# A RoPE kernel: rows of 16 KB instead of 64 KB where the DMA queue first goes over from loads to stores

## The chip, the cores and the metric

One core of one Trainium2 chip. The metric is the device time of one execution in microseconds (us), as the median of several runs. Lengths of rows are counted on the fp32 side (HBM) unless bf16 is said.

## The reference

```python
x: (8, 2048, 16, 64) fp32; cos, sin: (2048, 32) fp32
x1, x2 = x_pairs[..., 0], x_pairs[..., 1]        # neighbours along the last axis
out1 = x1 * cos - x2 * sin
out2 = x1 * sin + x2 * cos
out = stack([out1, out2], -1).reshape(x.shape)   # fp32
```

Eight batches, each 8 MB in and 8 MB out. There is little arithmetic for each byte.

## The kernel before

Each partition holds 16 consecutive sequence positions (`K = 16`) of a batch, 1024 elements each, so one partition's part of a batch is one contiguous run of 64 KB in HBM. Loads cast fp32 to bf16 and stores cast back. Every big transfer is issued by GpSimd, and they all go through one software queue, in the order of issue. There are three load buffers and three store buffers.

```python
P, K, KP, NX, NO, HEAD, TAIL = 128, 16, 8, 3, 3, 2, 4
x_t   = x.rearrange("b (p k) h d -> b p k (h d)", p=P, k=K)
out_t = out.rearrange("b (p k) h d -> b p k (h d)", p=P, k=K)

def load(b, k0=0):
    if b not in xs:
        xs[b] = xpool.tile([P, K, HD], bf16, name="xt")
    nc.gpsimd.dma_start(out=xs[b][:, k0:], in_=x_t[b, :, k0:])

def store(b, k1=K):
    nc.gpsimd.dma_start(out=out_t[b, :, :k1], in_=os[b][:, :k1])

# ... start: two positions of batch 0 and the tables by the other queues, then
load(0, HEAD)
load(1)
# ... tables are expanded on VectorE
load(2)
for b in range(B):
    os[b] = opool.tile([P, K, HD], bf16, name="ot")
    for k0 in range(0, K, KP):
        rotate(b, k0, k0 + KP)          # three tensor_tensor on VectorE
    if b + NX < B:
        load(b + NX)
    store(b, K if b < B - 1 else K - TAIL)
# ... the last four positions of the last batch leave by another queue
```

So the queue holds four loads (L0 to L3), then S0, L4, S1, L5, S2, L6, S3, L7, S4, S5, S6, S7. A place where a load is followed by a store is called a turn below; L3 to S0 is the first in this kernel. Each of the 16 DMA engines carries 8 partitions, which are 8 rows of 64 KB in each load or store.

## Time and profile before

| | before |
|---|---|
| median of 3 runs (range) | 317.47 us (317.31 to 317.48) |
| span of the profiled run | 315.7 us |
| VectorE busy | 212.8 us, 67% |
| DMA engines busy with the software queue | 97.0% |
| HBM bytes read and written over the span | 427 GB/s |

These are lines of the page of the kernel before: busy time by engine, the DMA rows of the 40 slices (a 9 means at least 90% busy), and one line of the queue table.

```profile
DVE 212.8 (67%) x51; ACT 6.9 (2%) x4; POOL 8.8 (3%) x20
...
DMA  9999999999999999999999999999999999999996
GB/s 269 212 246 203 199 212 253 199 199 237 361 465 332 199 257 407 399 332 262 203 399 440 357 199 199 482 448 266 199 316 415 399 399 523 407 399 457 423 434 280
...
q0 software_dynamic: 2304, 98.04, 97.0%
```

The DMA engines never rest, and VectorE does. The bytes are given, so all that can be won is time in which the engines are busy without moving data at their rate. To find such time, look at the table of stretches. Its columns are: the stretch and its length in us, the busy time of VectorE, ScalarE and GpSimd with the number of instructions, the granted clock, and then the two that matter here, the DMA share and the GB/s. **How to read these two:** a packet (one row) is counted with its whole length in the stretch in which it begins. If the stretch is one cadence long (2.40 us, the time from the start of one row to the start of the next) and one row of each engine begins in it, then share times length is the mean length of these rows. GB/s counts the bf16 side of a load and the fp32 side of a store, so 218 and 437 are the same speed.

```profile
core 0: us, DVE busy (x) ACT busy (x) POOL busy (x), PEclk, DMA share, GB/s
76.10:78.50 2.40, 2.40 (x2) 0.00 (x0) 0.00 (x0) 1.00 1.01 218
78.50:80.90 2.40, 2.40 (x1) 0.00 (x0) 1.05 (x2) 1.00 1.32 218
80.90:81.70 0.80, 0.80 (x1) 0.00 (x0) 0.00 (x0) 1.00 0.00 0
118.00:120.40 2.40, 2.40 (x2) 0.00 (x0) 0.00 (x0) 1.00 1.01 218
120.40:122.80 2.40, 2.37 (x2) 0.00 (x0) 0.00 (x0) 1.00 1.02 437
```

The seventh row of L3, which begins at about 76 us, takes 1.01 × 2.40 = 2.42 us, as all rows do. Its eighth and last takes 1.32 × 2.40 = 3.17 us, and where the next packets should begin, from 80.9 to 81.7 us, none does. That is 0.74 us lost per engine at the first change from loads to stores. At the next such change (L4 to S1, at about 120.4 us) the last row of the load takes 2.42 us again.

The list of issues and landings says the same. Its last column is the time from issue to landing; the load was issued at 52.20 us and the store at 52.72 us, so they landed at 82.8 and 102.2 us.

```profile
xt<-in_x_dram POOLq DMA_DIRECT2D x1, 4096.0 KB, 30.6
out_dram<-ot POOLq DMA_DIRECT2D x1, 49.5
```

### The profile page before, as it was taken

The numbers are of one execution on the slowest core, as the hardware profiler recorded it, in microseconds if no ns is written. First come the engines' busy times: TensorE is split into PE (matmuls) and PEld (weight loads), VectorE is DVE, ScalarE is ACT, GpSimd is POOL, SyncE is SP. The second block draws the span as 40 slices with busy tenths as digits, with TensorE's granted clock in tenths as the row PEclk, the third lists the DMA queues.
The fourth block names the chain that finished last, engine by engine and source line by source line (L and its number), as shares of the span: only waits on it lengthen the run. The fifth ranks groups of instructions, "written<-read, shape, count | busy, mean of one in ns | idle before, by whom it ended". The sixth has DMA issues, their size and how long they took to land.

```text
span 315.7 us, 146 instructions
## 1 busy us (share of the span) xinstructions
DVE 212.8 (67%) x51; ACT 6.9 (2%) x4; POOL 8.8 (3%) x20
## 2 busy tenths in 40 slices
DVE  0009999999999999619992299913999049990000
ACT  2100000000000000000000000000000000000400
POOL 1000001000100100100001000000000000000000
DMA  9999999999999999999999999999999999999996
GB/s 269 212 246 203 199 212 253 199 199 237 361 465 332 199 257 407 399 332 262 203 399 440 357 199 199 482 448 266 199 316 415 399 399 523 407 399 457 423 434 280
DMA packets 3024, 101.71 MB, mean 322 GB/s; under 512 B 336, under 2 KB 336, under 8 KB 848
## 3 DMA queue, kind: packets, MB, share of 16 engines
q0 software_dynamic: 2304, 98.04, 97.0%
q1 hardware_dynamic: 432, 2.88, 2.4%
q10 hardware_dynamic: 288, 0.79, 0.6%
HBM read 67.63 MB, written 67.11 MB: 427 GB/s over the span
## 4 chain that ended last, share of the span: by engine, by line
another core or an unknown queue 61%; DMA 16%; DVE 9%; ACT 1%; issue 0%; POOL 0%; ACTq 0%
DMA out_dram<-ot 16%; DVE xt L76 3%; DVE ot L81 3%; DVE ot L75 3%; ACT xt L117 1%; DVE c_tab L100 0%; POOL xt L57 0%; ACTq L116 0%; ACT ot L116 0%; ACTq L117 0%
## 5 line engine op out<-in xcount | busy, mean ns | idle before, releaser
L75 DVE TENSOR_TENSOR ot<-xt,c_tab 128x8192 bf16<-128x8192 bf16 x16 | 70.7, 4420 | 45.8 <-DMA out_dram<-ot 45.7
L81 DVE TENSOR_TENSOR ot<-ot,xt 128x8192 bf16<-128x8192 bf16 x16 | 70.8, 4425 | 0.5
L76 DVE TENSOR_TENSOR xt<-xt,s_tab 128x8192 bf16<-128x8192 bf16 x16 | 70.8, 4425 | 0.5
L98 DVE CAST s_tab<-xt 128x512 bf16<-128x512 f32 x1 | 0.5, 454 | 23.8 <-DMA xt<-in_sin_dram 23.8
L57 POOL DMA_DIRECT2D xt<-in_x_dram x8 | 4.4, 547 | 161.4 <-DVE ot L81 137.4
L60 POOL DMA_DIRECT2D out_dram<-ot x8 | 4.3, 535 | 113.8 <-DVE ot L81 113.8
L116 ACT COPY ot<-ot 1x1 bf16<-1x1 bf16 x1 | 0.2, 193 | 286.6 <-DMA out_dram<-ot 286.6
L117 ACT CAST xt<-ot 128x4096 f32<-128x4096 bf16 x1 | 3.6, 3604 | 0.0
L96 ACT CAST xt<-xt 128x2048 bf16<-128x2048 f32 x1 | 1.9, 1897 | 0.0
L96 ACT ACT_TABLE_LOAD x1 | 1.3, 1283 | 5.7 <-DMA xt<-in_x_dram 5.7
L100 DVE CAST c_tab<-xt 128x1024 bf16<-128x1024 f32 x1 | 0.7, 683 | 0.0
L99 DVE TENSOR_SCALAR s_tab<-xt 128x512 bf16<-128x512 f32 x1 | 0.4, 442 | 0.0
L133 POOL MEMSET const-float32-0.0<- 128x1 f32 x1 | 0.1, 98 | 0.2 <-issue 0.2
L133 POOL MEMSET const-bfloat16-1.0<- 128x1 bf16 x1 | 0.1, 101 | 0.0
L133 POOL MEMSET const-float32-1.0<- 128x1 f32 x1 | 0.1, 98 | 0.0
L133 POOL MEMSET const-uint8-127<- 128x1 uint8 x1 | 0.1, 98 | 0.0
## 6 DMA issues: line engine op xcount, KB each, us to landing
xt<-in_x_dram POOLq DMA_DIRECT2D x7, 4096.0 KB, 42.8
out_dram<-ot POOLq DMA_DIRECT2D x1, 6144.0 KB, 28.0
xt<-in_x_dram POOLq DMA_DIRECT2D x1, 3584.0 KB, 22.8
out_dram<-xt SPq DMA_DIRECT2D x1, 2048.0 KB, 15.5
xt<-in_x_dram ACTq DMA_DIRECT2D x1, 512.0 KB, 5.0
xt<-in_x_dram SPq DMA_DIRECT2D x1, 512.0 KB, 4.9
xt<-in_sin_dram ACTq DMA_DIRECT2D x1, 256.0 KB, 22.7
xt<-in_cos_dram SPq DMA_DIRECT2D x1, 256.0 KB, 18.3
```

The source lines that it names most:

```text
L57: nc.gpsimd.dma_start(out=xs[b][:, k0:], in_=x_t[b, :, k0:])
L60: nc.gpsimd.dma_start(out=out_t[b, :, :k1], in_=os[b][:, :k1])
L75: nc.vector.tensor_tensor(out=rows(op), in0=rows(xp), in1=tab(c_tab), op=mult)
L76: nc.vector.tensor_tensor(out=rows(xp), in0=rows(xp), in1=tab(s_tab), op=mult)
L81: nc.vector.tensor_tensor(out=o3, in0=o3, in1=x_swap, op=add)
L96: nc.scalar.copy(out=xs[0][:, :HEAD], in_=pre[:, :HEAD])
L98: nc.vector.tensor_copy(out=s2[:, :, 0], in_=sin_sb)
L99: nc.vector.tensor_scalar_mul(s2[:, :, 1], sin_sb, -1.0)
L100: nc.vector.tensor_copy(out=c_tab.rearrange("p k (i j) -> p (k i) j", j=2), in_=cos_sb.to_broadcast([P, K * D2, 2]),)
L116: nc.scalar.copy(out=os[B - 2][:1, 0, :1], in_=os[B - 1][:1, K - 1, :1])
L117: nc.scalar.copy(out=tail[:, :TAIL], in_=os[B - 1][:, K - TAIL :])
L133: nc = _bacc.Bacc("TRN2", target_bir_lowering=False, num_devices=1)
```

## The change

The intent: at that change, give the engines small rows, so that whatever is lost over the length of a row is lost over a shorter one. L3 ends and S0 begins with four positions (16 KB) of each partition, as transfers of their own.

```diff
+    TURN = 4
-    def load(b, k0=0):
+    def load(b, k0=0, k1=K):
...
-        nc.gpsimd.dma_start(out=xs[b][:, k0:], in_=x_t[b, :, k0:])
+        nc.gpsimd.dma_start(out=xs[b][:, k0:k1], in_=x_t[b, :, k0:k1])
-    def store(b, k1=K):
-        nc.gpsimd.dma_start(out=out_t[b, :, :k1], in_=os[b][:, :k1])
+    def store(b, k0=0, k1=K):
+        nc.gpsimd.dma_start(out=out_t[b, :, k0:k1], in_=os[b][:, k0:k1])
...
-            if b + NX < B:
-                load(b + NX)
-            store(b, K if b < B - 1 else K - TAIL)
+            if b == 0:
+                load(NX, 0, K - TURN)
+                load(NX, K - TURN)
+                store(0, 0, TURN)
+                store(0, TURN)
+            else:
+                if b + NX < B:
+                    load(b + NX)
+                store(b, 0, K if b < B - 1 else K - TAIL)
```

## The prediction

> **What bounds the kernel.** The DMA engines. The DMA row of the 40 slices reads 9 nearly throughout, and the queue table gives 97% of sixteen engines' span to the software queue that carries all big loads and stores. VectorE is busy 67% (212.8 us) and from the fifth batch on waits for stores to land (45.7 us). In the table of stretches, one row's time inside a store moves 437 GB/s, inside a load 218 counted on the bf16 side, so 436 on the fp32 side. The Trainium skill, "DMA: Bandwidth & Descriptors", section "Where 436 GB/s comes from", puts the ceiling at 435.2 GB/s; this trace agrees. Only bubbles are left to win.
>
> **Where a bubble is.** Loads land at 43.3, 62.6 and 82.8 us, the first store at 102.2; afterwards a landing follows every 19.25 us (loads) or 19.39 us (stores). The fourth load, which ends at the first turn from loads to stores, takes 20.2 us: 0.9 us too much. In the packet records its rows take 2.43 us each, but the last takes 2.81 to 3.52 us on the sixteen engines (mean about 3.14). In the table of stretches no packet begins from 80.9 to 81.7 us, where the cadence of 2.41 us would have had them begin. Later turns (near 120.5 us) show no longer row. So the loss comes once: 0.7 us in the mean engine, 0.9 in the last.
>
> My reading: the same page, section "Two DMAs through the same engine are not ordered", says that an engine's read and write sides are separate queues and descriptors are pipelined. The read of the store's first row starts before the load's last row is done and competes with it; then the loss scales with the rows at the turn. Why only at the first turn, the trace doesn't tell.
>
> **What the change does.** VectorE, ScalarE and SyncE keep their order. GpSimd issues two more large DMAs, about 0.53 us each, at 52 us, with ten microseconds of the third load still queued: off the path. Bytes are the same. Each engine gets 8 rows of 48 KB and 8 of 16 KB for the fourth load, 8 of 16 KB and 8 of 48 KB for the first store, instead of 8 and 8 of 64 KB. The end of the kernel has 16 KB rows already, at a cadence of 0.607 us against a quarter of 2.412 = 0.603; two more completion packets cost 22 to 42 ns each. Estimated new cost: 0.1 us. The added semaphore waits are on DMAs that landed long before.
>
> If the loss shrinks with the row, 0.9 becomes about 0.2: net 0.6 us, all on the critical path, because the queue never runs dry and each later landing shifts with it. If the read-ahead is limited by bytes, or the loss is a one-time start-up of the write side, 0.1 us is lost. I give the first about 60%.
>
> **Prediction:** 317.0 us, range 316.5 to 317.7; faster by over 2%: 0.5%; within 2%: 99%; slower by over 2%: 0.5%.
>
> **Right if:** the fourth load's last 16 KB rows take at most about 0.9 us (normally 0.61), the load lands by about 82.2 us, the first store by 101.6, and all after is 0.5 to 0.6 us earlier at the same intervals. **Wrong if:** the last rows together still lose 0.9 us, or a stretch appears elsewhere (into the 48 KB rows, at the second turn).
>
> **What would make it wrong:** a fixed latency, or something else at 79 us (GpSimd issues DMAs at 78.7 and 79.2 us); small rows slower here than at the end; differences between chips or runs as large as the gain.

## The result

| | before | after |
|---|---|---|
| median of 6 runs each, same rounds | 317.48 us (317.31 to 317.61) | 317.46 us (317.26 to 317.62) |
| ratio | | 1.0000, 95% interval 0.9987 to 1.0013 |
| span of the profiled run | 315.7 us | 315.9 us |

The time is the same. The interval reaches 0.0013 × 317.5 = 0.4 us to each side, so the gain of 0.5 us that was forecast is not there.

The page of the changed kernel, the same lines as before:

```profile
DVE 212.8 (67%) x51; ACT 7.0 (2%) x4; POOL 9.9 (3%) x22
...
DMA  9999999899999999999999999999999999999997
GB/s 264 216 250 199 199 220 245 183 230 194 320 494 371 199 228 436 398 332 253 212 398 398 390 207 199 448 481 266 199 299 431 398 398 506 423 398 431 436 425 301
...
q0 software_dynamic: 2592, 98.04, 97.2%
```

The list of issues and landings of the changed kernel. The two parts of the load were issued at 52.17 and 52.68 us, the two of the store at 53.20 and 53.73 us:

```profile
out_dram<-ot POOLq DMA_DIRECT2D x1, 6144.0 KB, 48.7
xt<-in_x_dram POOLq DMA_DIRECT2D x1, 3072.0 KB, 25.0
out_dram<-ot POOLq DMA_DIRECT2D x1, 2048.0 KB, 34.7
xt<-in_x_dram POOLq DMA_DIRECT2D x1, 1024.0 KB, 30.4
```

The load has landed completely at 52.68 + 30.4 = 83.1 us (before: 82.8), the store at 53.73 + 48.7 = 102.4 us (before: 102.2). The end of the load is not earlier, and everything after it in the trace keeps its old intervals of 19.25 and 19.39 us.

The table of stretches shows where the time is now. The columns are as before:

```profile
74.40:76.20 1.80, 1.80 (x1) 0.00 (x0) 0.00 (x0) 1.00 1.02 218
76.20:78.60 2.40, 2.40 (x2) 0.00 (x0) 0.00 (x0) 1.00 1.02 212
78.60:79.40 0.80, 0.80 (x1) 0.00 (x0) 0.73 (x2) 1.00 1.18 184
79.40:81.40 2.00, 2.00 (x1) 0.00 (x0) 0.33 (x1) 1.00 0.92 127
81.40:82.05 0.65, 0.65 (x1) 0.00 (x0) 0.00 (x0) 1.00 0.97 202
82.05:84.50 2.45, 2.42 (x2) 0.00 (x0) 0.00 (x0) 1.00 1.08 438
```

The 48 KB rows run within 0.07 us of full speed, all eight together, up to 76.2 us, and the first four 16 KB rows at full speed, to about 78.6 us. Then the rate falls: to 127 GB/s, 58% of 218, from 79.4 to 81.4 us. Before the first store packet begins at 82.07 us the load is already back at full speed: in the packet records the last 16 KB row of each engine takes its normal 0.625 us (at most 0.63), and the seventh 0.71 us on average, while the sixth of the eight took 1.09 to 1.31 us. Added up over the 16 KB rows, the packet records have 0.87 us of excess per engine, against 0.73 us in the last row before the change. So smaller rows made the loss visible in finer steps, and they did not make it smaller. And the slow stretch does not lie beside the turn: it begins about 3 us, or three to four rows of 16 KB, ahead of it. Before the change its place within the one long row could not be seen.

### The profile page after: what moved, and what is told of

It is laid out like the page before. It is cut to its first block, busy times and chain, and to the rows that moved or that the text cites. A ratio compares the mean times of both kernels' runs of the same rounds, so it can differ in the third digit from the quotient of the medians.

```text
span 315.9 us, 148 instructions
## 1 busy us (share of the span) xinstructions
DVE 212.8 (67%) x51; ACT 7.0 (2%) x4; POOL 9.9 (3%) x22
## 3 DMA queue, kind: packets, MB, share of 16 engines
q0 software_dynamic: 2592, 98.04, 97.2%
## 4 chain that ended last, share of the span: by engine, by line
another core or an unknown queue 91%; ACT 2%; DMA 2%; issue 0%; ACTq 0%
DMA xt<-in_x_dram 2%; ACT xt L125 1%; ACT xt L97 1%; ACT L97 0%; ACT ot L124 0%; ACTq L124 0%; ACTq L125 0%; ACTq L97 0%
## 6 DMA issues: line engine op xcount, KB each, us to landing
xt<-in_x_dram POOLq DMA_DIRECT2D x1, 1024.0 KB, 30.4
```

## The experiments

All are built from the kernel before unless it is said otherwise, and all gave correct results. "Loss" below is the excess length of a row per engine, from the DMA share: (share − share of an undisturbed row) × length of the stretch.

Four theories were on the table:

- **A, read-ahead:** an engine reads the first rows of the store while the last bytes of the load are still on their way, and these bytes come in at the cost of the load. It happens once, because the engine keeps the lead that it wins in the first store.
- **B, issue:** GpSimd issues L4 and S1 at 78.7 and 79.2 us. The slow stretch coincides with this in both kernels.
- **C, clock time:** something happens at 79 us of every execution.
- **D, start-up:** the first store of a queue costs a start-up, whatever its size.

### late_issue: the two issues at 79 us moved away

```diff
+    gate = consts.tile([P, 1], bf16)
...
                 rotate(b, k0, k0 + KP)
+                if b == 2 and k0 == 0:
+                    nc.gpsimd.tensor_copy(out=gate[:1, :1], in_=os[b][:1, 0, :1])
+                    load(4)
+                    store(1)
+            if b == 1:
+                continue
```

> The fifth load and the second store are issued at about 91.7 us instead of 78.7 and 79.2; the queue still has the first store to do until 102 us, so it does not run dry. Theory A (read-ahead: the engines' read side begins the first store's rows while the last bytes of the load are still coming in, for the first time only, because a lead won in the first store is kept afterwards): the slow stretch stays at the end of the fourth load, which still takes about 20.2 us, last rows 2.8 to 3.5 us. Theory B (the two issues of GpSimd at 78.7 and 79.2 us disturb the transfers): the fourth load takes 19.3 us, all its rows 2.43 us, and slow rows, if any, are near 92 us. Theory C (something at 79 us of every execution, whatever the queue does): still at 79 us. Total time within 0.3 us of before under A and C.

Measured, by the table of stretches of this run:

```profile
78.50:80.90 2.40, 2.40 (x1) 0.00 (x0) 0.00 (x0) 1.00 1.45 218
80.90:81.70 0.80, 0.80 (x1) 0.00 (x0) 0.00 (x0) 1.00 0.00 0
```

The last row of L3 took 1.45 × 2.40 = 3.48 us, a loss of 1.06 us, with no GpSimd instruction near. Theory B falls. The time of one run was 317.67 us.

The issues came at 96.0 us and not at 91.7 as expected. The timeline (start, length, engine, line, operation) shows why:

```profile
91.58 4.42 DVE L76 TENSOR_TENSOR ot<-xt,c_tab 128x8192 bf16<-128x8192 bf16 x1
91.73 4.31 POOL L111 COPY gate<-ot 1x1 bf16<-1x1 bf16 x1 [38.47 <-DVE ot L82]
95.98 0.53 POOL L58 DMA_DIRECT2D xt<-in_x_dram  x1
```

A copy of one element took 4.31 us, just as long as the VectorE multiplication beside it. The Trainium skill, "SBUF — State Buffer", section "Who interferes with whom", says that "A DVE instruction with two SBUF inputs contends with a GpSimd instruction that reads SBUF"; this trace agrees. It did no harm here, since the queue had work until 102 us.

### store_first: the turn moved forward

```diff
+            if b == 0:
+                store(b)
             if b + NX < B:
                 load(b + NX)
-            store(b, K if b < B - 1 else K - TAIL)
+            if b > 0:
+                store(b, K if b < B - 1 else K - TAIL)
```

> The first store is issued before the fourth load, so the queue turns to stores after the third load, near 62.6 us, and the load follows the store. Theory A: the third load takes about 20.2 us instead of 19.3, its last rows 2.8 to 3.5 us, landing at about 63.4 us; no slow row near 79 us; the turn before the second store shows none. Theory B or C: the third load takes 19.3 us and the rows running at 79 us are slow. Total time the same as before within 0.3 us under all.

Measured (stretches: the last rows of L2, and the rows that run at 78 us):

```profile
56.80:59.20 2.40, 2.40 (x1) 0.00 (x0) 0.00 (x0) 1.00 1.01 218
59.20:61.60 2.40, 2.37 (x2) 0.00 (x0) 0.00 (x0) 1.00 1.26 218
61.60:62.20 0.60, 0.60 (x1) 0.00 (x0) 0.00 (x0) 1.00 0.00 0
78.00:80.40 2.40, 2.40 (x2) 0.00 (x0) 1.05 (x2) 1.00 1.02 437
```

The last row of L2 lost (1.26 − 1.01) × 2.40 = 0.60 us, and at 79 us nothing is slow. The loss goes with the first turn, so theory C falls. The time was 317.59 us against 317.47, ratio 1.0004, interval 0.9988 to 1.0021: the same.

### tiny_store: a first store of 64 KB near the beginning

```diff
         load(0, HEAD)
+        tiny = consts.tile([P, 128], bf16)
+        nc.vector.memset(tiny, 0.0)
+        nc.gpsimd.dma_start(out=out_t[0, :, 0, :128], in_=tiny)
         load(1)
```

The real store overwrites these zeros later.

> A store of 64 KB in all (512 B per partition, zeros, overwritten by the real store later) goes into the queue right behind the first load. Theory A: too few bytes to win a lead, so the fourth load still takes about 20.2 us and its last rows 2.8 to 3.5 us; the first load loses at most some 0.1 us at its end. Theory D (the first write to HBM of a queue costs a start-up once, whatever its size): the first load's last rows stretch by about 0.7 us and the fourth load takes 19.3 us. Theory C: slow rows at 79 us still.

Measured (stretches: the last row of L0, ahead of the tiny store, and the last two of L3):

```profile
20.80:22.90 2.10, 0.00 (x0) 0.00 (x0) 0.00 (x0) 1.00 1.04 226
76.40:78.80 2.40, 2.40 (x2) 0.00 (x0) 0.05 (x1) 1.00 1.02 218
78.80:81.20 2.40, 2.40 (x1) 0.00 (x0) 1.00 (x2) 1.00 1.32 218
```

The last row of L0 was undisturbed. It is a row of 56 KB that takes 2.13 us; a few small packets of another queue fall into the same stretch, hence 1.04. L3 lost (1.32 − 1.02) × 2.40 = 0.72 us as ever. Theory D falls. One run took 318.00 us.

### dry_queue: the queue made to run dry in the middle

```diff
+    gate = consts.tile([P, 1], bf16)
...
                 rotate(b, k0, k0 + KP)
+                if b == 4 and k0 == 0:
+                    nc.gpsimd.tensor_copy(out=gate[:1, :1], in_=os[b][:1, 0, :1])
+                    for c in (2, 3):
+                        load(c + NX)
+                        store(c)
+            if b in (2, 3):
+                continue
```

> The sixth load and the third store are held back by a one-element GpSimd copy until the first half of the fifth batch is done, about 154 us; the queue runs dry after the second store, from about 141 to 155 us, and starts again with a load, then a store. The fourth load still takes 20.2 us. Theory A: the lead is lost while the queue is empty, so the last rows of the sixth load stretch again to 2.8 to 3.5 us and this load takes about 0.7 to 0.9 us more than 19.3, apart from its start-up. Theory D (a start-up paid once by the first store): rows there stay at 2.43 us. Theories B and C: no second stretch either, or one near the issues at 154 us. Total time about 13 to 15 us longer than before.

Measured (stretches: the last rows of L3, then the last rows of L5, the first load after the pause):

```profile
76.10:78.50 2.40, 2.40 (x2) 0.00 (x0) 0.00 (x0) 1.00 1.01 218
78.50:80.90 2.40, 2.40 (x1) 0.00 (x0) 1.05 (x2) 1.00 1.42 218
175.20:177.60 2.40, 0.00 (x0) 0.00 (x0) 0.00 (x0) 1.00 1.01 218
177.60:180.00 2.40, 0.00 (x0) 0.00 (x0) 0.00 (x0) 1.00 1.52 218
180.00:181.00 1.00, 0.00 (x0) 0.00 (x0) 0.00 (x0) 1.00 0.00 0
```

L3 lost (1.42 − 1.01) × 2.40 = 0.98 us, and L5, after two whole stores had gone through the queue, lost (1.52 − 1.01) × 2.40 = 1.22 us at its turn to S2. After the pause the loss was back. The gate is not the reason: late_issue has the same kind of gate without a pause, and after its first turn no row was over 0.02 us too long. This is what A expects, and D doesn't. The pause was longer than expected: L5's first packet began at 160.0 us, because this copy too took 4.3 us beside VectorE, and the run took 339.41 us, 21.9 more.

### load_rows and store_rows: each half of the change alone

From the changed kernel:

```diff
load_rows
-                store(0, 0, TURN)
-                store(0, TURN)
+                store(0)
store_rows
-                load(NX, 0, K - TURN)
-                load(NX, K - TURN)
+                load(NX)
```

> The load half of the change alone: the end of the fourth load in 16 KB rows, the first store whole in 64 KB rows. Theory A with a read-ahead limited in bytes: as in the changed kernel, the slow stretch lies two to three rows of 16 KB ahead of the turn, about 0.7 to 1.0 us lost per engine in all, the fourth load 20.2 to 20.6 us. If the read-ahead were limited to one row of the store, the loss would be at least as large as before, since that row is 64 KB again.

> The store half of the change alone: the fourth load whole in 64 KB rows, the first store beginning with 16 KB rows. Theory A with a read-ahead limited in bytes: the last 64 KB row of the load takes 2.8 to 3.5 us as before, the load 20.2 us. If the read-ahead were limited to one row of the store (the reading of the prediction), the stretch would shrink to at most 8 KB of bf16, about 0.3 us, so rows of at most 2.75 us and a load of about 19.6 us.

Measured (stretches of load_rows, as those of the changed kernel):

```profile
76.20:78.60 2.40, 2.40 (x2) 0.00 (x0) 0.00 (x0) 1.00 1.03 215
78.60:79.40 0.80, 0.80 (x1) 0.00 (x0) 0.55 (x2) 1.00 1.15 174
79.40:81.40 2.00, 2.00 (x1) 0.00 (x0) 0.51 (x1) 1.00 1.00 127
81.40:82.05 0.65, 0.65 (x1) 0.00 (x0) 0.00 (x0) 1.00 0.96 202
```

And of store_rows:

```profile
78.50:80.90 2.40, 2.40 (x1) 0.00 (x0) 1.06 (x2) 1.00 1.43 218
```

With the load in small rows the dip to 127 GB/s is the same, whether the store's rows are 16 KB (the changed kernel, 0.87 us lost) or 64 KB (load_rows, 1.04 us in the packet records). With the store in small rows, the last 64 KB row of the load lost (1.43 − 1.01) × 2.40 = 1.01 us. Had the engine read one row of the store ahead, as the prediction said, store_rows should have lost 0.3 us at most. The length of the store's rows does not set the loss. The single runs took 317.75 and 317.66 us.

### turn1: rows of 4 KB instead of 16 KB

```diff
-    TURN = 4
+    TURN = 1
```

> The changed kernel with 4 KB rows (TURN = 1) instead of 16 KB at the turn: eight rows of 4 KB and eight of 60 KB each way. Theory A with a read-ahead limited in bytes: the loss stays at 0.7 to 1.0 us per engine, now partly or wholly in the 60 KB row that precedes, or spread over the 4 KB rows; time the same as before within 0.3 us. If the read-ahead is limited to a few rows, whatever their size, the loss falls under 0.3 us and the kernel is 0.4 to 0.6 us faster than before.

Measured (the stretch in which the last 60 KB row of L3 begins; undisturbed, its share is 2.28 / 2.30 = 0.99):

```profile
77.00:79.30 2.30, 2.30 (x2) 0.00 (x0) 0.31 (x1) 1.00 1.14 214
```

In the packet records this row lost 0.33 us per engine (mean 2.61 us, normally 2.28), and its 4 KB rows lost 0.35 us more, mostly the first of them: 0.68 us together, as ever. The time was 318.08 us against 317.46, ratio 1.0017, interval 1.0001 to 1.0034. So even rows of 4 KB don't shrink the loss, and this kernel is slower by a little; of that, an uneven stretch of the load at 66 to 71 us (0.2 us in the packet records) is a part.

### mid_store, store_8k, store_16k: how large must a store be to win the lead?

The tiny store again, with more bytes. Of each partition it writes 128 elements in tiny_store, 512 in store_8k, 1024 in store_16k and 2048 in mid_store; one engine then reads 2, 8, 16 or 32 KB of bf16. The diff is that of store_16k against tiny_store.

```diff
-        tiny = consts.tile([P, 128], bf16)
+        tiny = consts.tile([P, 1024], bf16)
-        nc.gpsimd.dma_start(out=out_t[0, :, 0, :128], in_=tiny)
+        nc.gpsimd.dma_start(out=out_t[0, :, 0, :1024], in_=tiny)
```

> As the tiny store, but with 8 KB per partition (1 MB in all, zeros, overwritten later) behind the first load, 32 KB of bf16 per engine to read. Theory A: enough to win the lead, so the last rows of the first load stretch by 0.5 to 0.9 us, the fourth load then takes about 19.3 us with rows of 2.43 us, and the three loads before it show no uneven rows. Total time about 2.4 us longer for the extra megabyte, and the loss is moved, not added. If the loss belonged to the first full store of data, the fourth load would still take 20.2 us.

> The early store of zeros again, sized between the two already run: 1 KB of bf16 per partition, 8 KB to read per engine (the tiny one had 2 KB, the one of 1 MB had 32 KB). If the loss at a turn is the time in which bf16 bytes of the store come in ahead of the load's last bytes, at about 27 KB per us (a 64 KB row takes 2.41 us), the first load's end loses about 8/27 = 0.3 us per engine and the fourth load's end what is left of 0.7 to 1.0, so about 0.4 to 0.7 us. If it is all or nothing, one of the two loses 0.7 to 1.0 us and the other nothing.

> The early store with 2 KB of bf16 per partition, 16 KB to read per engine. By the same count the first load's end loses about 16/27 = 0.6 us per engine and the fourth load's end 0.1 to 0.4 us. All or nothing: one of the two 0.7 to 1.0 us, the other nothing.

Measured (stretches: the last row of L0, ahead of the early store, and the last row of L3). First mid_store, in which the last row of L3 begins at 81.8 us, then store_8k, then store_16k:

```profile
21.00:23.10 2.10, 0.00 (x0) 0.00 (x0) 0.00 (x0) 1.00 1.37 229
...
81.60:84.00 2.40, 2.37 (x2) 0.00 (x0) 0.00 (x0) 1.00 1.01 218
```

```profile
20.90:23.00 2.10, 0.00 (x0) 0.00 (x0) 0.00 (x0) 1.00 1.05 228
79.00:81.40 2.40, 2.40 (x1) 0.00 (x0) 0.84 (x2) 1.00 1.14 218
```

```profile
20.80:22.90 2.10, 0.00 (x0) 0.00 (x0) 0.00 (x0) 1.00 1.11 227
79.00:81.40 2.40, 2.40 (x1) 0.00 (x0) 1.06 (x2) 1.00 1.01 218
```

| early store, bf16 read per engine | loss at the end of L0 | loss at the end of L3 | sum | time of the one run |
|---|---|---|---|---|
| none (before) | none | 0.74 us | 0.74 us | 317.43 us |
| 2 KB (tiny_store) | 0.0 us | 0.72 us | 0.7 us | 318.00 us |
| 8 KB (store_8k) | 0.02 us | 0.31 us | 0.3 us | 317.88 us |
| 16 KB (store_16k) | 0.15 us | 0.0 us | 0.15 us | 318.45 us |
| 32 KB (mid_store) | 0.69 us | 0.0 us | 0.7 us | 320.08 us |

(At the end of L0 the undisturbed share is 1.04, as in tiny_store. The zeros themselves cost a quarter of 2.41 us in 8 KB, half of it in 16 KB and 2.41 us in 32 KB.) mid_store did what A expects: the loss moved from L3 to L0. The count behind the other two expectations failed. It took the loss for the time in which the store's bytes come in, so it expected 0.3 us and 0.6 us at L0 and the rest at L3. (It took bf16 bytes at 27 KB per us, which is the rate of the fp32 side; at that of the bf16 side, 32 KB in 2.41 us, the expected losses double and fail by more. The bound of 0.3 us for store_rows becomes 0.6 us, still under the 1.01 us measured.) The losses do not add up to a fixed sum at all: with 16 KB the engine had its lead for 0.15 us.

### early_turn and early_piece: real data in place of the zeros

As soon as the first half of batch 0 is rotated (39 us), a part of S0 goes into the queue, ahead of L2. In early_turn this is half of S0, in early_piece one position of each partition: 512 KB of fp32, 16 KB of bf16 per engine. No byte is moved twice.

```diff
-    def store(b, k1=K):
-        nc.gpsimd.dma_start(out=out_t[b, :, :k1], in_=os[b][:, :k1])
+    def store(b, k1=K, k0=0):
+        nc.gpsimd.dma_start(out=out_t[b, :, k0:k1], in_=os[b][:, k0:k1])
...
-        load(2)
         for b in range(B):
...
                 rotate(b, k0, k0 + KP)
+                if b == 0 and k0 == 0:
+                    store(b, 1)          # early_turn: store(b, KP)
+                    load(2)
             if b + NX < B:
                 load(b + NX)
-            store(b, K if b < B - 1 else K - TAIL)
+            store(b, K if b < B - 1 else K - TAIL, 1 if b == 0 else 0)    # early_turn: KP
```

> No extra bytes: half of the first store is issued as soon as the first half of the first batch is done (39 us) and ahead of the third load, so the first turn comes after the second load, at about 43 us, with real data. Theory A: the second load's last rows stretch by 0.6 to 1.0 us, no later row is uneven, since loads behind the first store have kept the lead; the loss is moved, and at most the unevenness of the third and fourth loads (0.0 to 0.2 us in the traces so far) is won. Time within 0.3 us of before, so same; a gain of more than 0.5 us would show that the turn can be made cheaper by its place.

> As the early turn with real data, but the piece of the first store that goes ahead is one row of 4 KB per partition (16 KB of bf16 to read per engine) instead of half the batch; the third load follows it and the rest of the store comes later, no extra bytes. From the early stores of zeros: with 16 KB per engine the end of the load before it lost 0.15 us and the fourth load's end nothing, against 0.7 to 1.0 us at a full turn. If that holds with real data, the second load's end loses 0.1 to 0.3 us, no later load row is uneven, and the time is 0.4 to 0.8 us under before (about 316.8 us). If the small loss with 16 KB belonged to the zeros or to the place behind the first load, the loss is 0.6 us or more at the second load's end or at the fourth load's turn, and the time is that of before.

Measured (stretches: the last row of L1, at the new turn). First early_turn, then early_piece, with the last row of L3, which now begins at about 80 us, as its second line:

```profile
39.90:42.30 2.40, 2.40 (x1) 0.00 (x0) 0.27 (x1) 1.00 1.28 218
```

```profile
39.30:41.70 2.40, 2.40 (x1) 0.00 (x0) 0.57 (x2) 1.00 1.09 218
79.60:82.00 2.40, 2.40 (x1) 0.00 (x0) 0.02 (x1) 1.00 1.01 218
```

| | time | before in the same rounds | ratio, 95% interval | loss at the end of L1 |
|---|---|---|---|---|
| early_turn | 317.56 us (317.00 to 317.66, 5 runs) | 317.48 us (9 runs) | 0.9997, 0.9984 to 1.0011 | 0.65 us |
| early_piece | 316.95 us (316.76 to 317.19, 5 runs) | 317.54 us (9 runs, lowest 317.38) | 0.9983, 0.9969 to 0.9997 | 0.19 us |

early_piece is 0.6 us faster than the kernel before: all its runs lie under all of the other's. It was not timed beside the changed kernel, but that one equals the kernel before (317.46 against 317.48 us), and the fastest of its six runs, 317.26 us, is over the slowest of early_piece. In one respect early_turn and early_piece differ, the size of the piece (and with it the length of its rows, 4 KB against 32 KB), and the loss at the turn falls from 0.65 to 0.19 us, which is most of the difference in time. The short rows are not the reason: in turn1 S0 begins with just such rows, eight of 4 KB for each engine, and 0.68 us was lost. In turn1 more of the store follows behind them, in early_piece a load. All these runs fit that the loss depends on how much store stands in the queue before the next load. The gain is small, 0.2%, but the interval leaves out 1.

## Why the prediction was right, and where it was not

- **What bounds the kernel: right.** The DMA engines are, at 97% before and 97.2% after. The time fell where a loss in the queue fell (early_piece), and it rose where bytes were added (mid_store) or the queue stood empty (dry_queue).
- **Where the bubble is: right in size** (0.74 us in the mean engine, 0.73 in the packet records) and in its connection with the first turn (store_first, late_issue).
- **"Then the loss scales with the rows at the turn": this step failed.** It carried the forecast of 0.6 us and was given 60%. The loss stayed at 0.87 us with 16 KB rows, 0.68 us with 4 KB rows, 1.01 us with small rows of the store alone. In undisturbed order it was 0.74, 0.98 and 1.06 us in three traces with 64 KB rows (before, dry_queue, late_issue), so these differences are within what it varies by. The other branch of the prediction, that "the read-ahead is limited by bytes" and nothing is gained, is the one that the result followed; a limit in bytes as such was not shown.
- **The signs for right and wrong worked.** The rows took up to 1.31 us instead of at most 0.9, the load landed at 83.1 and not 82.2 us, the store at 102.4 and not 101.6.
- **"Why only at the first turn, the trace doesn't tell": the runs do, in part.** After a store of at least 16 KB of bf16 per engine, later turns are free (store_16k, mid_store, early_turn, early_piece); after one of 8 KB about half of the loss is left (store_8k), after one of 2 KB all of it (tiny_store); and after a pause of the queue the loss came back (dry_queue, one run). This fits a state that an engine holds while its queue is never empty. The traces have a second sign of it: up to the first larger store, rows of loads are now and then 0.03 to 0.2 us too long (in the changed kernel at 59 to 75 us, in turn1 at 66 to 71 us), and after it not one row of a load is, in any of these traces, until the pause in dry_queue (rows over 0.02 us longer than the median of their size were counted).
- **The two added issues of GpSimd are off the path: right.** Its busy time rose from 8.8 to 9.9 us, and the queue had work all the while.
- **The estimated cost of the new rows, 0.1 us,** is too small to be told apart from the way the loss varies from run to run.
- **The number was right for its width, not for its reason.** 317.46 us lies in the range of 316.5 to 317.7, but so does the 317.48 us of the kernel before: a change without any effect fell within the range. The middle of it, 317.0 us, stood for a gain that did not come.

What stays open: that the state is a lead of the read side over the write side fits all runs, but the packet records hold one time per packet and do not show reads apart from writes, so the mechanism is argued and not shown: any other state that a store of 16 KB sets up and a pause clears would leave the same records. A turn here is also a change of the cast, from fp32 to bf16 and back, and no run tells the two apart. A lead of the reads could explain that the slow stretch comes ahead of the turn: the Trainium skill, "HBM Reference", section "Latency", gives 2 us for HBM under high load, and reads would have to be asked for that much earlier. That would be 2 of the about 3 us, and no run here measures that latency. Open too is why a piece of 16 KB wins the lead for 0.15 to 0.19 us while 32 KB and more cost 0.60 us and up; early_piece beside turn1 says only that it matters whether a load or more of the store stands behind the piece.

## What to carry to other kernels

A bubble beside a change of direction need not be about the size of the pieces at that place: a finer grain first of all shows where in time the loss lies, and here it lay 3 us ahead of the turn and was untouched by the grain. Before you shrink the pieces, move the suspected cause (the turn, the issue, the state of the queue) and see what the loss follows. In this queue a small store (16 KB of bf16 per engine) put early between two loads made the later turns free and cost 0.15 to 0.2 us instead of 0.6 to 1.1 us. In the one run in which the queue ran dry, the loss came again.

## What the Trainium skill lacked or had wrong

- "DMA: Bandwidth & Descriptors", section "Two DMAs through the same engine are not ordered": it says that descriptors are pipelined, but not that a queue's first change from loads to stores cost 0.60 to 1.06 us of the mean engine's time here, that later changes were free while the queue was never empty, and that after a pause of 19 us the cost came back with 1.22 us. No page has this.
- The same page, "Rules for kernel authors", advises at least 1 MiB per DMA for the highest bandwidth. It lacks an exception: here a piece of 512 KB taken out of an 8 MB store made the kernel faster, 316.95 us against 317.54, for the loss at the turn fell to 0.19 us.
